# New cost numbers and block-border numbers for the planner that orders a two-layer encoder kernel on one TensorE-bound core

## The chip, the core and the metric

The kernel runs on one core of one Trainium2 chip. The metric is device time in microseconds (us) of one launch; lower is better. Three timed executions of the kernel before gave 1086.05, 1087.27 and 1087.64 us; the median is 1087.27 us.

A core has five engines with a queue of instructions each: PE (TensorE, matrix multiply; its weight loads are shown as PEld), DVE (VectorE), ACT (ScalarE), POOL (GpSimd) and SP (SyncE, which here only issues DMAs). Engines run side by side and wait for each other through semaphores. Within one engine, instructions run in the order in which they stand in its queue.

## What is computed

A trunk of two residual layers on a (512, 1024) float32 input, each with an RMS norm ahead of it, and one more RMS norm at the end:

```python
def even_layer(h, ...):          # layer 0
    xa, ba, ca, za, ub, vb, zb = split(h @ w_in)
    ya = short_conv_branch(xa, ba, ca, conv_w) * silu(za)
    yb = chunked_sgu_branch(ub, vb, ...) * silu(zb)
    return concat([ya, yb]) @ w_out

def odd_layer(h, ...):           # layer 1
    pc, zc, fd, zd = split(h @ w_in)
    yc = rwkv7_bidir_branch(pc, ...) * silu(zc)
    yd = fourier_branch(fd, fnet_w) * silu(zd)
    return concat([yc, yd]) @ w_out

def wkv7_step(state, inp):       # 512 positions, forward and backward, 16 heads of 64
    r, w, k, v, a, b = inp
    sa = einsum('ij,j->i', state, a)
    state = state * w + outer(sa, b) + outer(v, k)
    return state, einsum('ij,j->i', state, r)
```

## The kernel before, in words

**Arithmetic.** Large projections run as three rounded float32 matmuls: each operand is split into a high part `hh` and a low part `hl`, and high x high, high x low and low x high are summed (`mm3`, L551). One such matmul takes a 128x128 weight tile and 512 columns. Every weight block of 512 KB is loaded by SP into `wf_...` and split by two instructions in `splits` (L505): a cast makes the high half, on ACT or DVE, and a subtraction makes the low half, on POOL or DVE (`less`, with the gain `LO`).

**Layer 0** (up to about 455 us) is a row of such projections. **Layer 1** cuts the scan into 8 chunks of 64 positions for each of 8 pairs of heads (j = 0 to 7). For each j:
- `prep`, `half`: gates and scaled operands, on DVE, ACT and POOL;
- `scores`: three bursts of small matmuls (`sm`, `sa`, `sz`), masked by DVE and copied by ACT;
- `inverse`: a triangular inverse by blocks. PE has four bursts of 32x32 matmuls there: `iH` (64 matmuls, each float32 matmul is two records in the trace), then DVE adds a unit matrix to the result (`iHs`), then `iTT` (64) and `iTB` (32) need `iHs`; later `iG` (32) and `iTJ` (32);
- `fold`: `sp` (needs `iTT`, `iTJ`), copied to `pt`, and four bursts `sg`, which need `pt`; they are masked and copied into `gq`;
- `chain`: 8 steps of the scan. A step is one DVE multiply `X`, five to nine small PE matmuls into `pa` and eight into `py`; the next step's `X` needs `pa`.
Between these pieces the wide projections of layer 1 (`pd_k`, `pd_r`, `pd_v`, `pd_zc`, `pd_fd`, `pd_zd`) are laid in units of three matmuls, one `mm3` each. After the last step of the scan stand what is left of the output projection (`po`) and the final norm.

```python
        if op.eng == "PE" and op.mode != self.clock["mode"] and not s[3]:
            at += self.STAY
        if op.eng == "PE" and op.need > n and not op.glue:
            at = max(at, self.fetched.get(i + 1, t + self.FETCH) - op.cost * n / op.words)
```

The clock is used only while the program is built. [...] All instructions are recorded by one helper line (L401), so the profile's rows are told apart by tile names, not by lines.

## Time and profile before

| | |
|---|---|
| median of three timed executions | 1087.27 us (1086.05 to 1087.64) |
| the profiled execution's own time | 1090.07 us |
| its span, first to last instruction | 1088.3 us |
| PE, busy | 1024.3 us, 94%, 12024 matmul records |
| DVE, busy | 651.3 us, 60%, 1225 instructions |
| ACT, busy | 472.7 us, 43% |
| POOL, busy | 124.9 us, 11%, 155 instructions |
| DMA | 84 GB/s, mean over the span |

How to read it: the span is what the trace covers; the execution's own time is 1.8 us more, and 2.8 us over the median of the timed ones. PE is the busiest engine by far, so a microsecond in which PE has nothing to do, or runs slower, is where time can be won; an idle DVE or ACT costs nothing as such. "Busy" for PE counts a matmul from its start to its modelled end, and matmuls overlap, so costs on PE are better read from the distance between two starts.

### The profile page before, as it was taken

How to read it: one execution, taken by the hardware profiler on the slowest of the kernel's cores; microseconds unless marked ns; L12 is line 12 of the kernel's file. 1: busy time of each engine (PE TensorE's matmuls, PEld its weight loads, DVE VectorE, ACT ScalarE, POOL GpSimd, SP SyncE). 2: the span in 40 equal slices, each digit the busy share in tenths (PEclk: the TensorE clock that was granted, in tenths of full speed). 3: DMA queues.
4: the chain of work that ended last, by engine and by line, in shares of the span. 5: the costliest groups of instructions: out<-in, count | busy, mean ns of one | idle time of the engine just before them, and what ended most of it. 6: DMA issues, size and time to landing. Idle time of an engine off the chain costs nothing. (4 is left out here: it accounts for less than half of the span.)

```text
span 1088.3 us, 27301 instructions
## 1 busy us (share of the span) xinstructions
PE 1024.3 (94%) x12024; PEld 839.3 (77%) x12024; DVE 651.3 (60%) x1225; ACT 472.7 (43%) x795; POOL 124.9 (11%) x155
## 2 busy tenths in 40 slices
PE   7999999999999999998898999989988899999997
PEld 6988888888888888876676778767767677777776
DVE  6464444344343336895795858867793976864453
ACT  7232222222222125753565455744644736453253
POOL 1001210010110010220012101321021201110000
PEclk9999999999999999999998999989998999999999
DMA  8322222322223332332012011110121111154033
GB/s 286 105 73 94 81 94 98 97 97 97 96 96 124 130 116 98 100 105 89 8 46 89 3 42 61 49 52 21 41 71 41 60 39 48 60 172 131 30 107 117
DMA packets 32663, 91.51 MB, mean 84 GB/s; under 512 B 4896, under 2 KB 7712, under 8 KB 32544
## 3 DMA queue, kind: packets, MB, share of 16 engines
q1 hardware_dynamic: 32544, 89.77, 25.1%
q8 instruction: 94, 1.54, 0.6%
q14 instruction: 25, 0.20, 0.1%
HBM read 81.82 MB, written 7.86 MB: 82 GB/s over the span
## 5 line engine op out<-in xcount | busy, mean ns | idle before, releaser
L401 PE MATMUL pe<-w_e,yh 128*128 128x512 f32 x256 | 81.5, 398 | 0.0
L401 PE MATMUL sg<-ops 64*128 64x128 f32 x512 | 66.6, 294 | 7.2 <-ACT am L401 2.1
L401 PEld LDWEIGHTS sg<-ops 64*128 64x128 f32 x512 | 53.9, 196 | 17.1 <-issue 3.9
L401 PE MATMUL sg<-pt,am 64*128 64x128 f32 x512 | 60.5, 283 | 0.0
L401 PEld LDWEIGHTS pe<-w_e,yh 128*128 128x128 f32 x256 | 48.1, 188 | 11.6
L401 ACT COPY gq<-sg 128x256 f32<-128x256 f32 x64 | 23.2, 370 | 71.7 <-DVE gq L401 70.5
L401 PEld LDWEIGHTS sg<-pt,am 64*128 64x128 f32 x512 | 52.3, 195 | 0.0
L401 PE MATMUL pd_zc<-hh,w_zc 128*128 128x512 f32 x128 | 50.5, 437 | 1.3 <-DVE w_zc L401 1.3
L401 PE MATMUL pe<-w_e,yl 128*128 128x512 f32 x128 | 50.3, 393 | 0.0
L401 DVE TENSOR_TENSOR w_e<-wf_e,w_e 128x1024 fp32r<-128x1024 f32 (+1 forms) x19 | 20.0, 1074 | 48.0 <-ACT w_e L401 47.8
L401 PE MATMUL pd_r<-hh,w_r 128*128 128x512 f32 x128 | 45.5, 409 | 2.0 <-DVE w_r L401 2.0
L401 DVE TENSOR_TENSOR gq<-sg,c_masks 128x256 f32<-128x256 f32 x64 | 25.6, 416 | 33.7 <-PE sg L401 33.7
L401 PE MATMUL pd_k<-hh,w_k 128*128 128x512 f32 (+1 forms) x144 | 44.6, 372 | 0.0
L401 PEld LDWEIGHTS pa<-X,gq 128*64 128x64 f32 x448 | 30.8, 139 | 17.1 <-issue 3.9
L401 ACT CAST w_e<-wf_e 128x1024 fp32r<-128x1024 f32 (+1 forms) x19 | 16.9, 913 | 62.4 <-PE pe L401 54.6
L401 PE MATMUL pd_v<-hh,w_v 128*128 128x512 f32 x128 | 43.8, 410 | 0.0
L401 PE MATMUL pa<-X,gq 128*64 128x64 f32 x448 | 38.8, 230 | 4.6 <-DVE X L401 2.0
L401 PE MATMUL pa<-c_cen,vq 128*64 128x128 f32 x256 | 42.6, 288 | 0.0
L401 PE MATMUL pd_ub<-hh,w_ub 128*128 128x512 f32 x128 | 40.5, 393 | 0.0
L401 PE MATMUL pd_zb<-hh,w_zb 128*128 128x512 f32 x128 | 40.4, 392 | 0.0
L401 PE MATMUL pd_xa<-hh,w_xa 128*128 128x512 f32 x128 | 40.4, 392 | 0.0
L401 PE MATMUL pd_ca<-hh,w_ca 128*128 128x512 f32 x128 | 40.4, 392 | 0.0
(362 smaller groups left out, 2831.4 us busy)
## 6 DMA issues: line engine op xcount, KB each, us to landing
wf_e<-in_w_eo SPq DMA_DIRECT2D x16, 512.0 KB
wf_o<-in_w_oo SPq DMA_DIRECT2D x12, 512.0 KB
wf_pv<-in_w_ev SPq DMA_DIRECT2D x8, 512.0 KB
wf_ub<-in_w_e SPq DMA_DIRECT2D x8, 512.0 KB
wf_zb<-in_w_e SPq DMA_DIRECT2D x8, 512.0 KB
wf_xa<-in_w_e SPq DMA_DIRECT2D x8, 512.0 KB
wf_ca<-in_w_e SPq DMA_DIRECT2D x8, 512.0 KB
wf_za<-in_w_e SPq DMA_DIRECT2D x8, 512.0 KB
```

Of the source, the lines that this page charges most:

```text
L401: i = op.call(*op.a, **op.kw)
```

## The change

Only numbers of the planner change. The instructions and their operands are the same in number on PE (7720 matmuls, 12024 records); a few casts, copies and subtractions go to another engine, and the order changes on every engine from the first microseconds on.

```diff
--- before.py
+++ after.py
@@ -128,13 +128,13 @@
                 self.cost = n / 2250
             else:
                 self.cols *= 4
-                self.cost = n / (600 if aps[1].shape[0] > 64 else 1200) if m == P else 2 * max(m, n) / 1200 / {(P, 64): 1.7, (P, 32): 4, (64, 64): 4, (64, 32): 3}.get(self.mode, 2.5)
+                self.cost = n / (600 if aps[1].shape[0] > 64 else 1040) if m == P else 2 * max(m, n) / 1200 / {(P, 64): 1.75, (P, 32): 4, (64, 64): 3.9, (64, 32): 5}.get(self.mode, 3)
         elif eng == "Pool":
-            self.cost = 0.06 + n / {"tensor_tensor": 300, "tensor_scalar_mul": 228, "tensor_copy": 300}.get(name, 985)
+            self.cost = 0.06 + n / {"tensor_tensor": 300, "tensor_scalar_mul": 228, "tensor_copy": 900}.get(name, 985)
         else:
             more = sum(math.prod(x.shape[1:]) == 1 < n for x in self.ins) - (self.ins[0].space == PSUM if self.ins else 0) / 2
             rate = 500 if name in ("transpose", "tensor_tensor_scan") else 960
-            self.cost = {"DVE": 0.07 + n / rate + 0.06 * math.ceil(more), "ACT": 0.1 + n / 1200 + 0.09 * more, "SP": max(0.5, 0.06 + n / 720)}[eng]
+            self.cost = {"DVE": 0.1 + n / rate + 0.06 * math.ceil(more), "ACT": 0.14 + n / 1200 + 0.09 * more, "SP": max(0.5, 0.06 + n / 720)}[eng]
 
         banks = [(x.tensor.name, "bank") for x in self.outs + self.ins if x.space == PSUM]
         self.keys = [self.where(x) for x in self.outs] + [banks], [self.where(x) for x in self.ins]
@@ -162,10 +162,10 @@
 
 
     TICK, WINDOW, BUSY, SOFT = 3.413, 3.2, 4500.0, 2600.0
-    BLOCK, FIRST, READ, FETCH = 256, 178, 33, 3.6
-    SAFE, URGE, SWITCH, STAY, COLD = {}, 0.5, 0.2, 0.15, 2400.0
+    BLOCK, FIRST, READ, FETCH, MORE = 256, 194, 42, 3.6, 1 / 300
+    SAFE, URGE, SWITCH, STAY, COLD = {}, 0.5, 0.1, 0.0, 2800.0
     GIVE = {"PE": 0.15, "ACT": 0.1, "DVE": 0.15, "Pool": 9.0, "SP": 9.0}
-    SAME = {"DVE": 0.13, "ACT": 0.14, "Pool": 0.1}
+    SAME = {"DVE": 0.1, "ACT": 0.14, "Pool": 0.1}
     LATE = {"": 0.2, "PE": 0.25, "ACT": 0.2, "DVE": 0.3, "Pool": 0.3, "SP": 2.5}
 
     def __init__(self, tc, nc):
@@ -294,7 +294,7 @@
 
     def fetch(self, op):
 
-        self.issued += op.words
+        self.issued += op.words * (1 + self.MORE)
         while self.issued + self.READ >= self.block * self.BLOCK + self.FIRST:
             self.block += 1
             self.fetched[self.block + 1] = max(self.clock["PE"], self.fetched.get(self.block, 0.0)) + self.FETCH
@@ -411,7 +411,7 @@
             self.fill(s)
 
 
-LO, SLACK, BURST, ORDER = 0.5, 2, 1, (("v", 1), ("zc", 1), ("k", 2), ("r", 2))
+LO, SLACK, BURST, ORDER = 0.8, 2, 1, (("v", 1), ("zc", 1), ("k", 2), ("r", 2))
 FIRST = (("r", 0), ("v", 0), ("fd", 0), ("zd", 0), ("k", 1), ("fd", 1), ("r", 1), ("zd", 1), ("zc", 0))
 EXTRA = {0: (("fd", 2),), 3: (("zd", 2),), 5: (("fd", 3),), 6: (("zd", 3),)}
 FR, HL, XN, HH = 4, 0.6, 0.4, 0.5
```

`fetch` now counts 1/300 of a word more for each word issued (`MORE`), and the border is taken at 194 instead of 178, the start of a fetch 42 words ahead of it instead of 33. `STAY` is 0, so a change of tile shape is no longer shunned, and `SWITCH` is halved. DVE and ACT instructions are taken to be 0.03 and 0.04 us longer, bursts with a 64-row stationary tile and 128 columns 15% longer, 64x32 tiles shorter. `LO` goes from 0.5 to 0.8.

Over the whole program, POOL has 15 instructions more than before (six more low halves of layer 1's weights, three more of layer 0's, six more of the small `ll` halves), DVE's count is equal in sum, and ACT has 15 fewer. Changes of tile shape from one PE instruction to the next rise from 278 to 343.

PE, j = 5, from the end of `sa` to `iTT` and what follows. `iH5` is the burst whose result DVE turns into `iHs5`, `iTT5` the burst that reads it, `pd_r6` a wide projection. Before:

```order
L401 MATMUL sa5_11_8509<-ops3_3213,at5_1_8017 64x128
L401 MATMUL iH5_8550<-iD5_8527,off_103 32x32 x64
L401 MATMUL iTT5_8676<-iHs5_8551,iDt5_8528 32x32 x64
L401 MATMUL pd_r6_8562<-hh_84,w_r6_8547 128x512
L401 MATMUL pd_r6_8562<-hl_85,w_r6_8547 128x512
L401 MATMUL pd_r6_8562<-hh_84,w_r6_8548 128x512
```

and now:

```order
L401 MATMUL pd_k6_8678<-hh_84,w_k6_8613 128x512
L401 MATMUL iH5_8732<-iD5_8705,off_103 32x32 x64
L401 MATMUL pd_r6_8726<-hh_84,w_r6_8680 128x512
L401 MATMUL pd_r6_8726<-hl_85,w_r6_8680 128x512
L401 MATMUL pd_r6_8726<-hh_84,w_r6_8681 128x512
L401 MATMUL pd_r6_8726<-hh_84,w_r6_8680 128x512
L401 MATMUL pd_r6_8726<-hl_85,w_r6_8680 128x512
L401 MATMUL pd_r6_8726<-hh_84,w_r6_8681 128x512
L401 MATMUL pd_r6_8726<-hh_84,w_r6_8680 128x512
L401 MATMUL pd_r6_8726<-hl_85,w_r6_8680 128x512
L401 MATMUL pd_r6_8726<-hh_84,w_r6_8681 128x512
L401 MATMUL iTT5_8807<-iHs5_8733,iDt5_8706 32x32 x64
```

Before, `iTT5` stood right behind `iH5`; now nine wide matmuls stand between the two.

PE, j = 1 to 2, three bursts of small matmuls. `iTB1` and `iG1` belong to the inverse of pair 1, `sm2` to the scores of pair 2, `pd_v2`, `pd_k2` and `pd_r2` are wide projections. Before:

```order
L401 MATMUL pd_v2_5041<-hl_85,w_v2_4970 128x512
L401 MATMUL pd_v2_5041<-hh_84,w_v2_4971 128x512
L401 MATMUL iTB1_5053<-iDt1_4764,iHs1_4795 32x32 x32
L401 MATMUL iG1_5209<-dz1_3218,mt1_4352 32x32 x32
L401 MATMUL sm2_0_5244<-at2_0_4951,ops0_3204 32x64
```

and now:

```order
L401 MATMUL iTB1_4909<-iDt1_4733,iHs1_4764 32x32 x32
L401 MATMUL pd_k2_4497<-hh_84,w_k2_4457 128x512
L401 MATMUL pd_k2_4497<-hl_85,w_k2_4457 128x512
L401 MATMUL pd_k2_4497<-hh_84,w_k2_4458 128x512
L401 MATMUL iG1_5045<-dz1_3224,mt1_4247 32x32 x32
L401 MATMUL pd_k2_4497<-hh_84,w_k2_4457 128x512
L401 MATMUL pd_k2_4497<-hl_85,w_k2_4457 128x512
L401 MATMUL pd_k2_4497<-hh_84,w_k2_4458 128x512
L401 MATMUL pd_r2_4822<-hh_84,w_r2_4784 128x512
L401 MATMUL pd_r2_4822<-hl_85,w_r2_4784 128x512
L401 MATMUL pd_r2_4822<-hh_84,w_r2_4785 128x512
L401 MATMUL iTJ1_5085<-iG1s_5078,iB1_5039 32x32 x32
```

Before, `iTB1`, `iG1` and the 64 matmuls of `sm2` stood one behind the other; now three to six wide matmuls stand after each burst, and `sm2` comes later.

POOL, the preparation of pair 4 (`w4`, `a4`: gates; `ll`: low half of the small weights; `bon3`, `y2`: sums of earlier pairs; `w_v4`, `w_zc4`, `w_r4`: low halves of weight blocks). Before:

```order
L401 TENSOR_SCALAR w4_0_6307<-w4_0_6307 128x512
L401 TENSOR_TENSOR bon3_6360<-bon3_6360,rq3_1_5776 128x512
L401 TENSOR_TENSOR ll_104<-lora4_1_6704,lh4_1_6706 64x128
L401 TENSOR_SCALAR a4_0_6308<-a4_0_6308 128x512
L401 TENSOR_SCALAR w4_1_6723<-w4_1_6723 128x512
L401 TENSOR_TENSOR y2_6672<-y2_6672,bon2_5250 128x512
L401 TENSOR_SCALAR a4_1_6724<-a4_1_6724 128x512
L401 TENSOR_TENSOR w_v4_6783<-wf_v4_6754,w_v4_6782 128x1024
L401 TENSOR_TENSOR w_zc4_6840<-wf_zc4_6824,w_zc4_6839 128x1024
```

and now:

```order
L401 TENSOR_SCALAR w4_0_6607<-w4_0_6607 128x512
L401 TENSOR_SCALAR a4_0_6608<-a4_0_6608 128x512
L401 TENSOR_TENSOR ll_104<-lora4_1_6667,lh4_1_6669 64x128 x2
L401 TENSOR_TENSOR w_r4_6697<-wf_r4_6618,w_r4_6696 128x1024
L401 TENSOR_TENSOR bon3_6660<-bon3_6660,rq3_1_6040 128x512
L401 TENSOR_SCALAR w4_1_6708<-w4_1_6708 128x512
L401 TENSOR_SCALAR a4_1_6709<-a4_1_6709 128x512
L401 TENSOR_TENSOR w_v4_6795<-wf_v4_6742,w_v4_6794 128x1024
L401 TENSOR_TENSOR w_zc4_6930<-wf_zc4_6842,w_zc4_6929 128x1024
```

`w_r4` and a second `ll4_1` have come to POOL from DVE; `y2` has gone further ahead.

## The prediction

> **What bounds the kernel now.** I read the page first, for the engine that has least to spare, and then busy time by stage (columns: stretch and length in us; busy us and records of PE, PEld, DVE, ACT, POOL; granted clock; DMA share; GB/s).

> ```profile
> span 1088.3 us, 27301 instructions
> PE 1024.3 (94%) x12024; PEld 839.3 (77%) x12024; DVE 651.3 (60%) x1225; ACT 472.7 (43%) x795; POOL 124.9 (11%) x155
> ```
> ```profile
> 0.00:455.00 455.00, 447.49 (x2222) 377.73 (x2223) 211.12 (x290) 150.67 (x211) 41.88 (x47) 1.00 0.33 111
> 455.00:537.00 82.00, 72.94 (x1159) 56.44 (x1159) 61.64 (x117) 40.67 (x70) 11.79 (x20) 0.96 0.24 77
> 537.00:1036.00 499.00, 458.34 (x8446) 368.52 (x8446) 355.92 (x783) 258.77 (x476) 69.90 (x88) 0.97 0.18 58
> 1036.00:1088.00 52.00, 45.53 (x202) 36.64 (x202) 22.66 (x37) 22.62 (x39) 1.28 (x1) 0.97 0.32 111
> ```

> PE bounds the kernel. In layer 0 (first row) it stands idle for 7.5 us of 455, at the start, at full clock: no order can win much there. After the last step of the scan (last row) only wide `po` matmuls are left, and the idle 6.5 us are the final norm and store. So the change is decided between 455 and 1036 us, where PE is idle for 9.1 + 40.7 = 49.8 us and its clock is below 1. I then asked for the groups of PE instructions and for its waits, to see what the idle time is (group: records | busy us, mean ns | idle before, and what ended it; wait: us in total, times, longest).

> ```profile
> L401 PE MATMUL iTT<-iHs,iDt 32*32 32x32 f32 x1024 | 11.1, 199 | 10.3 <-DVE iHs L401 7.5 <-DVE zz L401 2.4 <-issue 0.5
> L401 PE MATMUL iH<-iD,off 32*32 32x32 f32 x1024 | 10.8, 194 | 3.3 <-issue 3.3
> L401 PE MATMUL iTB<-iDt,iHs 32*32 32x32 f32 x512 | 7.2, 204 | 3.3 <-issue 3.3
> ```
> ```profile
> PE sg L401 <- ACT am L401: 2.1, 3, 1.4
> PE sm L401 <- issue: 1.8, 1, 1.8
> PE sg L401 <- ACT dz L401: 1.7, 2, 1.2
> PE bo L401 <- issue: 0.5, 1, 0.5
> ```

> Two causes stand out, both at bursts of 32-wide matmuls: "issue", in which PE waits for no engine (3.3 + 3.3 + 0.5 + 1.8 + 0.5 = 9.4 us), and `iTT` waiting for DVE's `iHs` and `zz` (9.9 us). The rest is some 20 small waits of up to 2.5 us.

> **The change, term by term.** The sum is made against the profiled execution (1090.07 us, 1.8 of it outside the span) and then taken off the median of 1087.27 us, 2.8 us lower. No instruction is added on PE, and SP's loads are the same, so each term is idle time, clock or tile-shape changes.

> *Block borders.* Here is one "issue" stall in the timeline (start, length, form, records).

> ```profile
> 589.41 0.72 PE L401 MATMUL iTB<-iDt,iHs 32*32 32x32 f32 x62
> 589.94 0.23 PE L401 MATMUL iG<-dz,mt 32*32 32x32 f32 x2
> 589.95 0.21 PE L401 MATMUL iTB<-iDt,iHs 32*32 32x32 f32 x2
> 589.97 0.75 PE L401 MATMUL iG<-dz,mt 32*32 32x32 f32 x62
> 590.65 1.22 PE L401 MATMUL sm<-at,ops 64*32 64x64 f32 x59
> 593.63 1.30 PE L401 MATMUL sm<-at,ops 64*32 64x64 f32 x69 [1.76 <-issue]
> ```
> ```profile
> q8 instruction: 94, 1.54, 0.6%
> ```

> 187 records pass in 2.5 us, then PE stands in the middle of `sm`. PE's instructions come in 94 blocks of 1.54 MB / 94 = 16 KB, 256 words. Counted in the trace, all seven such stalls stand at word 192 to 194 of a block if each record is two words and each wait-only instruction one: 33 x 256 + 193 here. The old table leaves the wait-only words out and puts the border 178 words into the count of matmul words alone: 8 words late here, 46 at the last stall. The burst it thinks it has fitted then crosses the true border before the block is there. Reckoned from the record 42 words ahead of the border before, five of the seven stalls end after 3.5 to 3.9 us (here 589.75 to 593.63), two after 5.1 and 6.0. So I lay the true borders over both orders, and for each take the PE work from that record to the next border, at the trace's distances between starts. Before, 13 pieces hold less than 3.6 us, with a shortfall of 14 us in all, of which 9.4 show as "issue" and the rest lies under other waits. In the new order six do, with 3.1 us in all (worst: 2.3 us ahead of the border behind `sm7`). In proportion that leaves 9.4 x 3.1 / 14 = 2.1; with the two slow fetches in mind I take 2.4 left: **-7.0** (bounds: -6.3, all 3.1 seen, and -9.4).

> [...]

> *`iTT` behind `iH`.*

> ```profile
> 506.31 1.29 PE L401 MATMUL iH<-iD,off 32*32 32x32 f32 x128
> 510.29 1.29 PE L401 MATMUL iTT<-iHs,iDt 32*32 32x32 f32 x128 [2.70 <-DVE iHs L401]
> ```
> ```profile
> 713.86 0.68 DVE L401 TENSOR_TENSOR iHs<-iH,c_eye 128x512 f32<-128x512 f32 x1
> 714.68 1.28 PE L401 MATMUL iTT<-iHs,iDt 32*32 32x32 f32 x128 [3.28 <-DVE iHs L401]
> ```

> In pair 0 nothing stood between the two bursts, and `iTT` came 2.7 us late; in pair 3 six wide matmuls did, and it was still 3.3 us late, because DVE had other work ahead of `iHs`. The new order lays 9 to 12 wide matmuls there in seven of eight pairs (2.3 to 3.0 us of PE work; pair 4 has 8.8). Pairs 0, 1 and 5 are covered by that; pair 3 would still lack about 2 us (3.3 less the 1.3 us by which its cover grows), and I leave 0.9 for the others: 9.9 - 2.9, **-7.0** (bounds: 0, if DVE is late by as much elsewhere, and -9.9).

> *Half clock.*

> ```profile
> core 0: 1088.3 us, clock 0.983
> ```
> ```profile
> 500.00:520.00 20.00, 16.61 (x574) 12.90 (x572) 7.76 (x13) 9.73 (x19) 0.00 (x0) 0.91 0.21 67
> 580.00:600.00 20.00, 17.56 (x483) 13.90 (x483) 7.82 (x16) 9.87 (x19) 4.40 (x7) 0.75 0.27 83
> 820.00:840.00 20.00, 15.87 (x480) 12.97 (x480) 4.79 (x10) 6.58 (x13) 2.73 (x3) 0.83 0.17 54
> ```

> 0.017 x 1088.3 = 18.5 us are lost to a lower granted clock; I take 17 of them to lie ahead of the final norm. Nearly every one stands where dense 32-wide bursts and one of the stalls above follow each other (510.3, 593.6, 714.7 in the rows above). With wide matmuls between the bursts and no stall, I take two in five of them to go: **-7.0** (bounds: 0 and -17).

> *Changes of tile shape.*

> ```profile
> 533.77 0.39 PE L401 MATMUL pd_k<-hl,w_k 128*128 128x512 f32 x1
> 534.00 0.40 PE L401 MATMUL pd_k<-hh,w_k 128*128 128x512 f32 x1
> 534.32 0.65 PE L401 MATMUL pa<-c_cen,vq 128*64 128x128 f32 x4
> ```

> A wide matmul holds PE for 0.23 us, but 0.32 if the next has another shape: a change costs 0.09 to 0.10. The new order has 343 for 278: 65 x 0.097 = 6.3 us. Some fall into time in which PE would wait anyhow: **+5.0** (bounds 0 and +6.3).

> *`sg` behind `sp`.* In the new order the work between `sp` and the first `sg` that reads its copy is 1.0 to 1.3 us in four pairs, where one pair had so little before. In the old order such short covers cost either nothing or some 0.9 us, within the rows of `sg` above. Five places by 0.4: **+2.0** (bounds 0 and +4.5).

> *More halves on POOL.* Below are DVE's timeline, POOL's at the same time, and DVE's group of such halves.

> ```profile
> 707.09 0.68 DVE L401 TENSOR_TENSOR ops<-kq,a 128x512 f32<-128x512 f32 x1
> 708.35 2.94 DVE L401 TENSOR_TENSOR ops<-rq,E 128x512 f32<-128x512 f32 x2
> ```
> ```profile
> 707.77 2.37 POOL L401 TENSOR_TENSOR w_zc<-wf_zc,w_zc 128x1024 fp32r<-128x1024 f32 x1 [6.40 <-ACT w_zc L401]
> ```
> ```profile
> L401 DVE TENSOR_TENSOR w_k<-wf_k,w_k 128x1024 fp32r<-128x1024 f32 x8 | 9.8, 1226 | 0.6 <-ACT w_k L401 0.4 <-issue 0.2
> ```

> The first `ops` takes 0.68 us; the two that meet POOL's half take 2.94, some 1.6 us more. Six more halves of layer 1 go to POOL: each spares DVE 1.2 us and may block it for 1.6. Bounds: -7.3 (none meets) to +2.4 (all meet) on DVE, of which PE sees a part. Since the blocked work stood just ahead of the `iHs` that PE waited longest for, I take it near the upper end: **+2.0**.

> [...] Were every added half blocked for its own 2.4 us, this term would be 6 x 1.2 = +7.

> Sum: -7.0 - 7.0 - 7.0 + 5.0 + 2.0 + 2.0 = -12.0 us. 1087.27 - 12.0 = **1075.3 us**, 1078.1 for a profiled execution.

> **Rivals.** *DVE sets the pace (1085).*

> ```profile
> 537.00:615.00 78.00, 69.97 (x1230) 55.05 (x1232) 63.26 (x143) 44.36 (x82) 16.28 (x20) 0.93 0.15 48
> 615.00:667.00 52.00, 49.57 (x1112) 40.95 (x1109) 35.04 (x72) 28.70 (x53) 3.68 (x7) 1.00 0.15 45
> 667.00:742.00 75.00, 69.42 (x1235) 54.83 (x1232) 61.68 (x140) 42.11 (x80) 18.59 (x20) 0.95 0.14 43
> ```

> These are the steps of pairs 0, 1 and 2. PE idles 8.0 and 5.6 us where DVE is busy for 81 and 82% of the time, 2.4 where it is for 67%. At the trace's mean durations the new order puts 71 and 69 us of DVE's work beside 74 us of PE's into pairs 2 and 4, and 30 to 46 beside 41 to 57 into the others. If DVE can't get past 82%, these two last 87 and 84 us, 23 over PE's work; five others at 2.4 and the last at 2 make 37, against 40.7 now. That is -3.7; with -2 of half clock, -2.7 of the first `iTT` ahead of 537 us and +6.3 of changes it comes to -2: 1085.

> *Changes cost, waits move (1092).* If the waits taken from `iTT` and the borders only come back at `X`, `sg` and `sp`, the new order pays 65 x 0.097 = 6.3 us for nothing, less some 1.5 at borders: 1092. It is the slower side, decided in the wide blocks that are now cut up between the steps of the scan; it wins if waits and half clock together shrink by less than 6.3 us. For it speaks that only 19.3 of 49.8 us of idle time have a cause that the new order visibly attacks.

> *The border table doesn't fit (1082).* Its drift of 1/300 adds 80 words over the program, the new queue holds 98 wait-only ones. If its bursts stall after all, the first term is lost: 1082.

> *All of it works (1062).* Borders -9.4, `iTT` -9.9, half clock -17, other waits -2, less 6.3 and 7 for `sg` and POOL at their worst comes to -25: 1062.

> **Chances.** Forecast 0.50, DVE's pace 0.18, changes cost 0.17, border table 0.05, all of it 0.10. Under 0.2% (2.2 us) a measurement of this kernel hardly tells a difference from none. Faster by more: forecast, all of it, border table, and 0.11 of DVE's pace: 0.76. Same: the other 0.07. Slower: 0.17. The range runs from 1062 to 1091, which leaves some 0.1 on each side; the forecast's own is 1067 to 1082.

> **What would show it.** In the new profile PE's "issue" waits should be under 3.5 us and its waits of `iTT` for `iHs` under 3; the mean clock should be 0.989 or more; PE's idle time between the scan's first and last step should be under 34 us. DVE's pace shows as PE waiting for DVE in the steps of pairs 2 and 4; POOL's part as DVE's `ops` or `iA` over 1.5 us beside `w_...` halves. I am wrong if idle time stays at 41 us, or if new waits at `X`, `sg` or `sp` exceed 6 us.

## The result, and the profile after

The median falls from 1087.42 to 1061.81 us (1059.61 to 1063.80, four executions): a ratio of 0.977, interval 0.974 to 0.979, or 25.6 us. The direction was forecast, the size was not: -12 was the forecast, and the time is that of the rival in which all of it works (1062), though not by that rival's sum. Two of the later executions, one of only_border (1258 us) and one of no_vec (1242 us), ran at a mean clock of 0.75 and are left out of every figure below.

The first lines of the page after, then busy time by stage (columns as before; the scan's steps now run from 539 to 977 us, and ran from 537 to 1036), and the granted clock:

```profile
span 1061.9 us, 27323 instructions
PE 1020.0 (96%) x12024; PEld 823.1 (78%) x12024; DVE 661.5 (62%) x1225; ACT 470.7 (44%) x780; POOL 150.9 (14%) x170
```
```profile
0.00:455.00 455.00, 445.32 (x2213) 375.61 (x2214) 210.95 (x285) 148.84 (x206) 51.56 (x50) 1.00 0.33 111
455.00:537.00 82.00, 74.16 (x1163) 55.19 (x1163) 70.64 (x129) 44.77 (x77) 30.58 (x34) 0.96 0.23 78
537.00:977.00 440.00, 425.56 (x8324) 332.23 (x8321) 339.33 (x746) 241.49 (x441) 67.17 (x86) 1.00 0.17 57
977.00:1062.00 85.00, 74.98 (x334) 60.05 (x332) 40.62 (x67) 35.58 (x58) 1.58 (x1) 0.98 0.35 115
```
```profile
core 0: 1061.9 us, clock 0.994
```

Layer 0 is nearly as it was (idle for 9.7 us, 7.5 before). In the scan PE stands idle for 440.00 - 425.56 = 14.4 us, where it was 40.7, and its clock there is 1.00 for 0.97; the 82 us ahead of the scan, idle for 7.8, now lose more for each us than the scan does. The scan ends 59 us earlier, but not all of that is won: more of `po` is left for the stage behind it, which grows from 52 to 85 us and is idle for 10.0 us instead of 6.5. Over the whole span PE's idle time falls by some 22 us. The list of PE's waits shows what is left (rows picked: those for no engine, and some of the largest others of layer 1):

```profile
PE iH L401 <- DVE iD L401: 2.6, 1, 2.6
PE sm L401 <- DVE ops L401: 2.4, 2, 1.3
PE zw L401 <- ACT E L401: 2.2, 1, 2.2
PE iG L401 <- issue: 2.1, 3, 1.1
...
PE iTT L401 <- issue: 1.5, 2, 1.2
PE sg L401 <- ACT gq L401: 1.5, 2, 1.0
...
PE iTJ L401 <- issue: 0.8, 1, 0.8
PE py L401 <- issue: 0.6, 1, 0.6
...
PE ss L401 <- issue: 0.4, 1, 0.4
PE sm L401 <- issue: 0.4, 1, 0.4
...
PE pa L401 <- issue: 0.3, 1, 0.3
PE sp L401 <- issue: 0.2, 1, 0.2
PE sg L401 <- ACT am L401: 0.2, 1, 0.2
```

"issue" adds up to 6.2 us (unrounded; 9.3 before). No row of `iTT` waiting for `iHs` or `zz` is left (9.9 before). And `sg`, which the prediction took to get worse, got better. Its group before and, in the second fence, after (busy us, mean ns of one | idle us ahead of the group, and what ended it):

```profile
L401 PE MATMUL sg<-ops 64*128 64x128 f32 x512 | 66.6, 294 | 7.2 <-ACT am L401 2.1 <-ACT dz L401 1.7 <-ACT gq L401 1.3
```
```profile
L401 PE MATMUL sg<-ops 64*128 64x128 f32 x512 | 55.6, 285 | 1.6 <-ACT gq L401 1.5 <-ACT am L401 0.2
```

This is pair 0 in PE's timeline after, the place where `iTT` waited 2.70 us before:

```profile
508.90 0.80 PE L401 MATMUL iH<-iD,off 32*32 32x32 f32 x35
509.64 0.80 PE L401 MATMUL pd_zc<-hh,w_zc 128*128 128x512 f32 x1
...
513.52 0.40 PE L401 MATMUL pd_zc<-hh,w_zc 128*128 128x512 f32 x1
513.85 1.22 PE L401 MATMUL iTT<-iHs,iDt 32*32 32x32 f32 x121
516.30 0.23 PE L401 MATMUL iTT<-iHs,iDt 32*32 32x32 f32 x4 [1.23 <-issue]
516.38 0.74 PE L401 MATMUL iTB<-iDt,iHs 32*32 32x32 f32 x62
```

Wide matmuls cover DVE's `iHs`, and `iTT` waits for no engine; but a block border, at record 121 of `iTT`, still costs 1.23 us.

Where the 26.4 us between the two spans went, by these views (changes of shape are reckoned, not seen as time lost: how the sum of the usual distances between PE's starts differs between the two orders):

| term | forecast | measured |
|---|---|---|
| block borders ("issue" 9.3 to 6.2) | -7.0 | -3.1 |
| `iTT` behind `iH` (9.9 to 0) | -7.0 | -9.9 |
| half clock (0.017 x 1088.3 = 18.5 to 0.006 x 1061.9 = 6.4) | -7.0 | -12.1 |
| changes of tile shape (278 to 343) | +5.0 | +6.4 |
| `sg` (7.2 to 1.6) | +2.0 | -5.6 |
| POOL, and all other waits for DVE and ACT (46.5 to 28.3 in all) | +2.0 | -2.7 |
| sum | -12.0 | -27.0 |

So the sum closes within 1 us. The reckoned row agrees with the traces: PE's busy time less half of what it works at half clock is 1024.3 - 32.1 / 2 = 1008.3 us before and 1020.0 - 9.8 / 2 = 1015.1 after, 6.8 more. Three questions are left. What takes `sg`'s and the other waits away? Do the borders do what was said of them? And how much of this belongs to the numbers, how much to the one order that came out of them?

### The profile page after: what moved, and what is told of

It is laid out like the page before. It is cut to its first block, busy times and chain, and to the rows that moved or that the text cites. A ratio compares the mean times of both kernels' runs of the same rounds, so it can differ in the third digit from the quotient of the medians.

```text
span 1061.9 us, 27323 instructions
## 1 busy us (share of the span) xinstructions
PE 1020.0 (96%) x12024; PEld 823.1 (78%) x12024; DVE 661.5 (62%) x1225; ACT 470.7 (44%) x780; POOL 150.9 (14%) x170
## 3 DMA queue, kind: packets, MB, share of 16 engines
q8 instruction: 94, 1.54, 0.6%
## 4 chain that ended last, share of the span: by engine, by line
PE 84%; DVE 10%; ACT 2%; issue 2%; DMA 1%; SPq 1%; POOL 0%; DVEq 0%; ACTq 0%; POOLq 0%
PE pe L401 8%; PE po L401 6%; PE sg L401 5%; PE pv L401 4%; PE pd_zb L401 4%; PE pd_ub L401 4%; PE pd_xa L401 4%; PE pd_ba L401 4%; PE pd_za L401 4%; PE pd_ca L401 4%; PE pd_v L401 4%; PE pd_k L401 4%; PE pd_r L401 4%; PE pd_zc L401 3%; PE pa L401 3%
## 5 line engine op out<-in xcount | busy, mean ns | idle before, releaser
L401 PE MATMUL pe<-w_e,yh 128*128 128x512 f32 x256 | 81.0, 397 | 0.0
L401 PE MATMUL sg<-ops 64*128 64x128 f32 x512 | 55.6, 285 | 1.6 <-ACT gq L401 1.5
L401 PEld LDWEIGHTS pe<-w_e,yh 128*128 128x128 f32 x256 | 48.0, 188 | 11.6
L401 PE MATMUL sg<-pt,am 64*128 64x128 f32 x512 | 51.8, 273 | 0.0
L401 PEld LDWEIGHTS sg<-ops 64*128 64x128 f32 x512 | 41.8, 187 | 11.7 <-issue 7.0
L401 PE MATMUL pe<-w_e,yl 128*128 128x512 f32 x128 | 50.4, 394 | 0.0
L401 PE MATMUL pd_k<-hh,w_k 128*128 128x512 f32 (+1 forms) x144 | 49.1, 395 | 0.9 <-DVE w_k L401 0.9
L401 DVE TENSOR_TENSOR w_e<-wf_e,w_e 128x1024 fp32r<-128x1024 f32 (+1 forms) x19 | 20.0, 1074 | 48.0 <-ACT w_e L401 47.8
L401 PE MATMUL pd_zc<-hh,w_zc 128*128 128x512 f32 x128 | 49.0, 419 | 0.0
L401 PE MATMUL pd_r<-hh,w_r 128*128 128x512 f32 x128 | 48.2, 416 | 0.0
L401 PE MATMUL pd_v<-hh,w_v 128*128 128x512 f32 x128 | 46.1, 406 | 0.0
L401 ACT COPY gq<-sg 128x256 f32<-128x256 f32 x60 | 22.0, 371 | 51.6 <-DVE gq L401 51.4
L401 ACT CAST w_e<-wf_e 128x1024 fp32r<-128x1024 f32 (+1 forms) x19 | 16.9, 912 | 62.4 <-PE pe L401 54.5
L401 PE MATMUL pa<-c_cen,vq 128*64 128x128 f32 x256 | 41.9, 285 | 0.0
L401 PEld LDWEIGHTS sg<-pt,am 64*128 64x128 f32 x512 | 41.7, 188 | 0.0
L401 PE MATMUL pd_ub<-hh,w_ub 128*128 128x512 f32 x128 | 40.8, 394 | 0.0
L401 PE MATMUL pd_zb<-hh,w_zb 128*128 128x512 f32 x128 | 40.7, 394 | 0.0
L401 PE MATMUL pd_xa<-hh,w_xa 128*128 128x512 f32 x128 | 40.5, 392 | 0.0
L401 PE MATMUL pd_ba<-hh,w_ba 128*128 128x512 f32 x128 | 40.4, 392 | 0.0
L401 PE MATMUL pd_ca<-hh,w_ca 128*128 128x512 f32 x128 | 40.4, 392 | 0.0
L401 PE MATMUL pd_za<-hh,w_za 128*128 128x512 f32 x128 | 40.4, 392 | 0.0
L401 PEld LDWEIGHTS pa<-X,gq 128*64 128x64 f32 x448 | 30.3, 137 | 12.9 <-issue 3.5
```

The source lines that it names most:

```text
L401: i = op.call(*op.a, **op.kw)
```

## The experiments

Each kernel is the one before or the change with a few planner numbers different, or the change's own order with one thing edited. In the table, "waits" is the sum of the list of PE's waits for DVE and ACT, "half clock" is (1 - clock) x span; both are of one profiled execution. The ratio is of timed executions to those of the kernel before on the same chip. The kernel before itself had medians from 1087.4 to 1089.8 us on these chips, so small differences between rows are read from the ratios.

| kernel | ratio (interval) | median us | waits | issue | half clock | changes |
|---|---|---|---|---|---|---|
| before | | 1087.4 | 46.5 | 9.3 | 18.5 | 278 |
| the change | 0.977 (0.974-0.979) | 1061.8 | 28.3 | 6.2 | 6.4 | 343 |
| only_shape | 0.990 (0.987-0.994) | 1077.0 | 26.4 | 14.1 | 11.8 | 334 |
| no_shape | 1.023 (1.019-1.028) | 1112.9 | 58.0 | 8.0 | 33.3 | 273 |
| only_border | 0.993 (0.991-0.995) | 1080.6 | 49.0 | 3.3 | 12.9 | 264 |
| no_border | 0.980 (0.977-0.983) | 1065.4 | 27.8 | 9.6 | 7.4 | 330 |
| shape_border | 0.986 (0.981-0.992) | 1071.5 | 27.4 | 6.5 | 11.7 | 337 |
| f_shift | 0.982 (0.979-0.986) | 1070.9 | 26.8 | 10.7 | 9.6 | 344 |
| f_pool | 0.971 (0.967-0.975) | 1056.0 | 20.9 | 6.2 | 5.3 | 343 |
| n_before | 1.003 (1.000-1.006) | 1090.8 | 45.5 | 10.0 | 22.9 | 274 |
| n_before315 | 0.999 (0.997-1.001) | 1086.8 | 48.0 | 4.1 | 16.3 | 271 |
| n_after | 0.996 (0.993-0.998) | 1084.5 | 37.5 | 8.5 | 18.4 | 336 |
| n_after315 | 0.989 (0.985-0.994) | 1077.4 | 28.7 | 9.3 | 13.9 | 332 |
| n_after33 | 0.973 (0.968-0.977) | 1057.6 | 23.8 | 4.0 | 5.3 | 338 |
| no_vec | 0.986 (0.981-0.991) | 1072.2 | 32.6 | 3.5 | 10.7 | 349 |
| no_pe | 0.971 (0.967-0.976) | 1056.6 | 25.6 | 3.8 | 7.4 | 343 |
| n33_pool | 0.968 (0.964-0.972) | 1052.9 | 21.4 | 6.9 | 3.2 | 338 |
| n325_pool | 0.991 (0.988-0.994) | 1078.3 | 29.9 | 13.3 | 12.9 | 336 |

### Tile-shape numbers alone, and all but them

only_shape, on the kernel before; no_shape puts the old two values back into the change:

```diff
-    SAFE, URGE, SWITCH, STAY, COLD = {}, 0.5, 0.2, 0.15, 2400.0
+    SAFE, URGE, SWITCH, STAY, COLD = {}, 0.5, 0.1, 0.0, 2400.0
```

> The kernel before with SWITCH 0.1 and STAY 0 alone; all other numbers as before. Laid over this order, the true block borders leave a shortfall of 2.6 us (14.0 before, 3.1 in the changed kernel), and every pair has 2.3 to 2.8 us of PE work between iH and iTT; 334 changes of shape. Theory A (the border numbers took the issue stalls away, accurate durations the other waits): shape alone gains under 6 us, 1081 or more. Theory B (letting PE change shape freely lays wide matmuls between the dense bursts, and that takes the issue stalls, the iTT waits and the half clock away): 1072 or less, issue under 4 us, clock 0.990 or more. Theory C (luck of the order): anywhere from 1075 to 1095.

> The changed kernel with SWITCH 0.2 and STAY 0.15 put back. Shortfall at the borders 13.9 us, 273 changes of shape, no work between iH and iTT of pair 0. Theory A: keeps most of the gain, 1070 or less, issue under 4 us. Theory B: loses most of it, 1080 or more, issue 7 us or more, clock 0.986 or less. Theory C: anywhere from 1065 to 1095.

Alone, the two numbers win 1% and take the waits from 46.5 to 26.4 us. With 1077 us and 14.1 us of "issue" the run fits neither theory A nor B, only the wide range of luck. Without them the rest of the change is 2.3% slower than the kernel before, as theory B had it, and beyond the range of luck: waits 58.0 us, half clock 33.3. These are rows of PE's waits in no_shape, two of the tiles being those that the prediction feared for (`sg` and `sp`):

```profile
PE sp L401 <- ACT ysq L401: 3.3, 1, 3.3
PE sg L401 <- ACT dz L401: 2.9, 2, 1.5
PE sp L401 <- ACT am L401: 2.2, 2, 1.9
PE sa L401 <- ACT pt L401: 1.8, 2, 1.3
```

So the waits go with the two tile-shape numbers, and the rest of the table agrees: 45.5 to 58.0 us in the five kernels without them, 20.9 to 37.5 in the thirteen with them. The reading of it, from the orders, is that a planner that shuns changes lays small bursts side by side, and each waits for the mask or copy that follows the one ahead of it. Which of the two numbers does it was not tried. Why the other numbers without these two are worse than none was not settled; it is one order, too.

### Border numbers alone, all but them, and with the shape numbers

only_border, on the kernel before (no_border takes the same out of the change; shape_border is the kernel before with both):

```diff
-    BLOCK, FIRST, READ, FETCH = 256, 178, 33, 3.6
+    BLOCK, FIRST, READ, FETCH, MORE = 256, 194, 42, 3.6, 1 / 300
...
-        self.issued += op.words
+        self.issued += op.words * (1 + self.MORE)
```

> The kernel before with FIRST 194, READ 42 and the drift of 1/300 alone. Shortfall 13.6 us, 264 changes of shape. Theory A: issue under 4 us, 1080 or less. Theory B: issue stays near 9 us, 1083 to 1091.

> The changed kernel with FIRST 178, READ 33 and no drift. Shortfall 4.0 us, 330 changes of shape. Theory A: 5 to 7 us of issue come back, 1067 to 1070. Theory B: within 4 us of the changed kernel's 1062, issue under 7 us.

> The kernel before with SWITCH, STAY and the border numbers, and with all durations, LO and COLD as before. Theory B with the borders added: the two parts make most of the gain, 1068 or less, issue under 7 us. If the measured durations of DVE, ACT and the small groups carry what was won beyond the prediction: 1070 to 1078, with ACT and DVE waits as in the run with shape alone (26 us together) or more.

With the border numbers "issue" falls from 9.3 to 3.3 us alone, and is 9.6 without them, 6.2 with them, in the change. With the shape numbers it is 14.1 without and 6.5 with them. In these three pairs of orders that is 3 to 8 us of "issue" and 0.4% to 0.7% of the time. It is not shown that the border numbers did it: other orders of the same numbers, further down, scatter about as widely (4.1 to 10.0 us of "issue" with the old border numbers, 4.0 to 9.3 with the new ones). Of the expectations, only_border had the "issue" of theory A (under 4) and just missed its time (1080 or less), no_border the time of theory B (within 4 us of 1062) but more "issue", and shape_border fell into the case in which something else carries the rest. The old kind of order keeps its other waits: this is only_border.

```profile
PE iTT L401 <- DVE iHs L401: 4.8, 2, 2.9
PE iG L401 <- ACT dz L401: 2.9, 2, 1.7
PE iTT L401 <- DVE zz L401: 2.2, 1, 2.2
```

Both groups together win 1.4%, of the change's 2.3%. What gives the other 0.9% is open: `LO`, `COLD` and POOL's duration were not put back one by one, and one order may be that much better than another by chance.

### The borders moved through one order

f_shift keeps the change's order of every instruction and puts 32 tiny matmuls (64 records, 128 words, under 1 us at the 1.29 to 1.93 us that 128 such records take) ahead of PE's first transposes, into a tile that these overwrite, so that every border falls half a block elsewhere.

```diff
+            if op.name == "transpose" and not self.issued:
+                for _ in range(32):
+                    o, y, e = (v[0:32, 0:32] for v in op.a[:3])
+                    self.tc.keep_in_program_order(self.engines["PE"].matmul(o, e, y, start=True, stop=True))
```

> The changed kernel in exactly its order, with 32 tiny 32x32 matmuls (64 records, 128 words) put ahead of the first transposes, so that every block border stands 128 words earlier in the work; the results are overwritten. The start grows by under 2 us. If borders decide by where they fall, 'issue' rises from 6.2 to 10 us or more and the time by 3 to 8 us over the changed kernel beside the start. If they hardly matter as long as wide work lies between the bursts, 'issue' stays within 2 us of 6.2 and the time within 2 us.

"issue" rises from 6.2 to 10.7 us and the span by 6.5, as expected if borders decide by where they fall. PE's timeline in pair 0 of f_shift, the piece shown above for the change:

```profile
514.52 1.27 PE L405 MATMUL iTT<-iHs,iDt 32*32 32x32 f32 x127
...
515.62 0.68 PE L405 MATMUL iTB<-iDt,iHs 32*32 32x32 f32 x56
519.18 0.26 PE L405 MATMUL iTB<-iDt,iHs 32*32 32x32 f32 x7 [2.88 <-issue]
```

The stall now comes 127 + 1 + 1 + 56 = 185 records into the bursts instead of 121. The 64 records that were put in bring every border 64 records forward, to 57, and the next one stands a block of 128 records behind it, at 185. In both kernels the stall ends 4.2 to 4.4 us after PE passed the border ahead; here all 128 records between the two borders are of dense bursts, so PE is through them sooner and waits longer (2.88 us for 1.23). So "issue" is the block border, shown at equal order.

### POOL's halves on DVE

f_pool keeps the change's order and issues the eleven low halves of layer 1's weights, which POOL computes there, on DVE:

```diff
-            i = op.call(*op.a, **op.kw)
+            call = op.call
+            if op.eng == "Pool" and op.name == "tensor_tensor" and re.match(r"w_(k|r|v|zc|fd|zd)\d", op.a[0].tensor.name):
+                call = self.engines["DVE"].tensor_tensor
+            i = call(*op.a, **op.kw)
```

> The changed kernel in its order, but the 11 low halves of layer 1's weights that the planner gave to POOL are issued on DVE at the same place. DVE gets 11 x 1.22 = 13.4 us of work more and POOL 26 us less. If POOL's halves block DVE about as long as they spare it (the prediction's term), the time changes by under 3 us either way. If they are real relief for DVE, it rises by 6 us or more, with PE's waits for DVE. If blocking costs more than it spares, it falls by 3 us or more.

Faster by 5.8 us by the medians and 0.6% by the ratios, as expected if blocking costs more than it spares, though DVE gets eleven instructions of 1.2 to 1.6 us more. DVE and POOL of the change, and then the same DVE instruction in f_pool (start, length):

```profile
850.33 2.29 DVE L401 TENSOR_TENSOR iA<-iA,iT 128x64 f32<-128x64 f32 x1
```
```profile
850.18 2.36 POOL L401 TENSOR_TENSOR w_k<-wf_k,w_k 128x1024 fp32r<-128x1024 f32 x1
```
```profile
843.21 0.22 DVE L404 TENSOR_TENSOR iA<-iA,iT 128x64 f32<-128x64 f32 x1
...
845.25 1.59 DVE L404 TENSOR_TENSOR w_k<-wf_k,w_k 128x1024 fp32r<-128x1024 f32 x1
```

A DVE instruction of 0.22 us takes 2.29 us and ends with POOL's half. Over the whole program, the time of DVE's instructions that overlap one of POOL's, above the median of the same form without overlap, sums to some 25 us before, 45 in the change and 27 in f_pool. The halves on POOL cost more than they spare.

### Is it the numbers, or the draw of one order?

`WINDOW`, the length over which the planner counts columns, stays put in the change. Moving it by 2 or 3% means nothing to the chip, but gives another order of the same kind. n_before and n_before315 do this to the kernel before, n_after, n_after315 and n_after33 to the change (3.25, 3.15 and 3.3):

```diff
-    TICK, WINDOW, BUSY, SOFT = 3.413, 3.2, 4500.0, 2600.0
+    TICK, WINDOW, BUSY, SOFT = 3.413, 3.25, 4500.0, 2600.0
```

> The changed kernel with one number that means nothing here set a little otherwise (WINDOW 3.25 for 3.2), which gives another order of the same kind: 336 changes of shape, 2.5 to 3.0 us between iH and iTT. If the gain lies in the kind of order, 1058 to 1070, clock 0.990 or more, ACT waits under 10 us. If it is luck of one order, 1070 or more.

> The kernel before with the number that means nothing (WINDOW 3.25 for 3.2): another order of the old kind, 274 changes of shape. If the kind of order decides: 1080 to 1105, half clock 14 us or more. If luck decides as much: it may reach 1070.

> The kernel before with WINDOW 3.15: a third order of the old kind, 271 changes of shape. If the kind decides: 1080 to 1105. If luck decides as much: it may reach 1070.

> The changed kernel with WINDOW 3.15: a third order of the new kind, 332 changes of shape, 2.9 to 3.0 us between iH and iTT. If the changed kernel's 1062 is a lucky draw of its kind: 1066 to 1086, half clock 10 us or more. If the kind gives it and WINDOW 3.25 was an unlucky draw: 1058 to 1066.

> The changed kernel with WINDOW 3.3: a fourth order of the new kind, 338 changes of shape. The same two cases as with 3.15: 1066 to 1086 if 1062 was a lucky draw, 1058 to 1066 if not.

The three orders of the old numbers lie within 4 us. The four of the new ones have ratios of 0.973, 0.977, 0.989 and 0.996: all faster, mean 0.984 (-18 us), spread over 25 us, which leaves the mean uncertain by some 6 us. Of the cases expected, n_after and n_after315 (1084.5 and 1077.4 us) say that the change's 1062 was a lucky draw, and n_after33 (1057.6) that it was not. In all four `iTT` waits for no engine; what differs is "issue", half clock and PE's waits, `iH` among them (2.6 us in the change, 4.8 to 7.2 in the others). This is the worst place in n_after (PE's timeline; then busy time and clock of that stretch):

```profile
902.92 1.93 PE L401 MATMUL iH<-iD,off 32*32 32x32 f32 x128 [4.20 <-DVE iD L401]
904.78 1.22 PE L401 MATMUL pd_v<-hh,w_v 128*128 128x512 f32 x2
...
914.40 0.66 PE L401 MATMUL sm<-at,ops 64*32 64x64 f32 x40
917.08 1.55 PE L401 MATMUL sm<-at,ops 64*32 64x64 f32 x88 [2.03 <-issue]
918.56 0.79 PE L401 MATMUL pd_v<-hh,w_v 128*128 128x512 f32 x1
```
```profile
900.00:920.00 20.00, 14.89 (x534) 12.01 (x535) 7.89 (x15) 5.17 (x9) 1.00 (x4) 0.67 0.21 69
```

`iH` waits 4.2 us, and behind it PE works at half clock: 128 records take 1.93 us where they take 1.29 at full clock, and wide matmuls stand 0.43 us apart for 0.23. Then three bursts side by side cross a border, with a stall of 2.03 us, and wide matmuls behind it stand 0.43 us apart again. One stretch of 20 us loses 5.1 us to waits and at most 6.6 to the clock (0.33 x 20; by the trace PE waits for some 4 us of the half-clock time anyhow, which leaves 4.6). Over the 18 kernels of the table a fit gives 0.59 us of half clock more for each us of PE's waits more, issue counted (correlation 0.92): by that, a wait taken away would be worth some 1.6 times its length. A fit of the span itself gives 1.3 us for each us of waits (correlation 0.97); the orders with fewer waits have more changes of tile shape, which may be why it is less. No run takes a single wait away, so this is how the two go together, not a price that was shown.

### Duration numbers, and POOL's halves in a good and a bad draw

no_vec and no_pe put the old durations of DVE and ACT, or of small PE groups, back into the change; n33_pool and n325_pool are n_after33 and n_after with the edit of f_pool.

```diff
-            self.cost = {"DVE": 0.1 + n / rate + 0.06 * math.ceil(more), "ACT": 0.14 + n / 1200 + 0.09 * more, "SP": max(0.5, 0.06 + n / 720)}[eng]
+            self.cost = {"DVE": 0.07 + n / rate + 0.06 * math.ceil(more), "ACT": 0.1 + n / 1200 + 0.09 * more, "SP": max(0.5, 0.06 + n / 720)}[eng]
...
-    SAME = {"DVE": 0.1, "ACT": 0.14, "Pool": 0.1}
+    SAME = {"DVE": 0.13, "ACT": 0.14, "Pool": 0.1}
```

> The change without its longer durations of DVE and ACT instructions (and with the old number for waits of one engine for itself). If these numbers carry the fall of PE's waits for DVE and ACT (29 us in the change, 46.5 before): such waits of 36 us or more and a time of 1075 to 1090. If they do not: waits of 22 to 33 us and a time within the scatter of the new kind about its middle, 1058 to 1075. Shortfall at block borders is 3.0 us by the order, so issue stalls of 4 to 9 us either way.

> The change with the old durations of small matmul groups. If the durations of small groups carry part of the gain: 1075 to 1090, with PE's waits for DVE and ACT at 36 us or more. If not: within 1055 to 1075, waits of 22 to 33 us. By the order alone its shortfall at block borders is the smallest seen (1.5 us), so issue stalls of 3 to 8 us.

> The change with the planner's window number at 3.3 (1057.6 us alone) and, in that exact order, the eleven low halves of layer 1's weights issued on DVE in place of POOL. [...] Rival (the gain seen in the order of the change was that order's own luck): within 2 us of 1057.6, or slower, since eleven halves of 1.2 us each are added to DVE.

> The same edit in the order of the window number 3.25 (1084.5 us alone, the slowest of the new kind; DVE's delay under POOL 48 us). Theory (a constant cost of POOL's halves): faster by 3 to 10 us, 1074.5 to 1081.5, and still at least 15 us slower than the good draw with the same edit, since its block borders and half clock stay. Rival (POOL's halves are what makes this draw slow): faster by 15 us or more, under 1069.5. Second rival (luck of one order): within 2 us of 1084.5 or slower.

Neither group of durations carries the fall of the waits: 32.6 us without the one, 25.6 without the other, both times in the ranges expected for that case and about the scatter of the new kind (no_pe is as fast as any order of the change without the POOL edit). The POOL edit gains 5.8, 4.7 and 6.2 us by the medians in three orders (6.3, 4.7 and 4.8 by the ratios; each is about as large as its interval, but all three agree), while the distance between a good and a bad draw stays: 1052.9 and 1078.3 with it, 1057.6 and 1084.5 without. So the halves on POOL are not what makes draws bad, and no difference in their cost between the orders is seen. In n33_pool and n325_pool (not in f_pool) "issue" rises with the edit (4.0 to 6.9 and 8.5 to 13.3 us), though PE's order and its borders are the same: where PE waits less for DVE, it comes to the next border sooner. That is a reading, not tried. n33_pool, 3.2% under the kernel before, is the fastest of all.

## Why the prediction fell short

**`sg` behind `sp`, and the waits that no term names: the step that failed.** The prediction counted in how many pairs the work between `sp` and the first `sg` had become short, and put +2.0 on it. Measured: 7.2 to 1.6, -5.6. All the waits that it doesn't name it left as they were; with POOL's term they were to be +2.0 and came out at -2.7. These two make 12.3 of the 15.0 us by which the sum missed. The count looked at one cover and missed that the copies `sg` waited for before (`am`, `dz`, `gq`) are covered too, once small bursts no longer stand side by side. The runs name what does it: the two tile-shape numbers alone take 20 us of waits away, PE's waits are low wherever these numbers are in, and `sg` waits for engines for 5.4 to 8.6 us in the five kernels without them and for 0.4 to 3.6 in the thirteen with them. The rival "changes cost, waits move" made the same error in words: it held it for a point that only 19.3 us of idle time have a cause that the new order visibly attacks.

**Half clock: right direction, too small.** Two in five of 17 us were put down to go; two in three went (-12.1). It was tied to the stalls named. The other waits fell as well, and over the 18 kernels half clock goes with all of PE's waits; that it fell because of them fits, but no run separates the two.

**`iTT` behind `iH`: right, and whole.** All 9.9 us went, for 7.0. The 2.9 us left for pair 3 and the rest did not come: DVE was done with `iHs` 0.7 to 1.8 us after the end of `iH` in every pair, where pair 3 took 4.8 before, and 9 to 12 wide matmuls cover that. DVE's own order has a part in it: in no_vec three pairs are late again (3.4 to 3.9 us), and `iTT` waits for 2.9.

**Block borders: the stall is real, the count of it is not borne out.** -3.1 for -7.0; 6.2 us of "issue" against the 2.4 expected and the 3.5 set as a mark. That the stalls stand at the true borders is right, as f_shift shows (6.2 to 10.7 us in the same order). The step that failed in this term is the fixed 3.6 us for a fetch: by that count only_shape should lose 2.6 us, and it lost 14.1. Over the eight orders whose count is on record, the shortfall counted and "issue" don't go together (13.6 and 3.3 us in only_border, 3.1 and 6.2 in the change). So this term's sign was in good part luck.

**Changes of tile shape** cost +6.4 for +5.0, by the reckoning above: nearly nothing fell into waiting time. **More halves on POOL** were rightly a cost. f_pool gives 5.8 us for eleven halves, so an estimate of 3 us for the six that were added, if each costs the same; in the measured sum this hides under waits that fell by more.

**Rivals.** These are the steps of pairs 2 and 4 after, where DVE's pace was to show:

```profile
642.00:725.00 83.00, 78.98 (x1404) 60.88 (x1404) 74.46 (x151) 48.45 (x85) 20.89 (x22) 0.98 0.18 56
769.00:850.00 81.00, 76.56 (x1390) 58.58 (x1388) 70.40 (x154) 46.88 (x81) 17.06 (x21) 1.00 0.18 58
```

DVE gets past the 82% at which that rival held it: 90 and 87% here, and PE idles for 4.0 and 4.4 us. Most of the scan's idle time is in these two pairs and the one behind them, but it is a third of the 23 us that the rival gave the two. Whether the border table fits stays open: "issue" is 6.2 us, between the 2.4 of the forecast and the 9.4 of that rival. What the prediction had no case for is the draw: its -12 stands beside a mean of -18 over four orders of these numbers, with single orders from -5 to -30. By that mean some 8 us of the 25.6 are this order's luck, give or take the 6 us by which four orders leave the mean uncertain; for the numbers as a kind, -12 is not ruled out.

**The marks.** Clock 0.994 (0.989 or more asked for), `iTT`'s waits for `iHs` 0 (under 3), idle time in the scan 14.4 us (under 34): met. "issue" 6.2 (under 3.5): missed. New waits at `X`, `sg` or `sp` of over 6 us did not come (`sg` 1.6 in all, `sp` none, `pa` for `X` 1.4). DVE's instructions beside POOL's halves: seen, at 2.29 us.

## What to carry to other kernels

When an order changes as a whole, price the waits that it doesn't name as well: take the tiles at which the critical engine waits now and look at what each has ahead of it in the new order, instead of leaving them as they are. Where waits and a lowered clock stand together, count a wait at more than its length (over the 18 kernels here the span went by 1.3 us with each us of waits). And before a gain is put down to a planner's numbers, nudge one that means nothing: here that moved the time by up to 27 us, as much as the change itself, and "issue" by more than 5 us.

## What the runs showed of the hardware

- **Blocks of instructions.** Queue q8 moved 94 pieces of 16 KB (1.54 MB), and in f_shift a stall stood 128 records behind the border ahead of it. The planner's fixed 3.6 us for a fetch was not borne out: in only_shape eleven of thirteen stalls ended 3.4 to 5.1 us after the border ahead of theirs (one after 5.8, one after 2.3), and the order, due 2.6 us of stalls by 3.6 us for each fetch, had 14.1. These times are worked out from the trace's records of single instructions and transfers. The longest stall there is 2.6 us, and 2.9 in f_shift. Before and after the change, all 18 of PE's stalls of 0.2 us or more that waited for no engine ended 1.2 to 1.5 us after the end of a q8 transfer.
- **Half clock** (a granted clock of 0.5), as the traces record it ahead of the final norm, came in pieces of 3.4 us or a multiple of it (before: four of 3.4 and three of 6.8; after: three of 3.4; in the other runs mostly 3.4, often 6.8, and 10.2 in n_after and in no_shape). Wide matmuls stood 0.43 us apart in them, 0.23 at full clock. In all 18 traces PE has a stall of 0.7 to 4.2 us in the 7 us ahead of each piece, often with bursts of 32-wide matmuls about it, but not always.
- **POOL and DVE.** Beside one 128x1024 subtraction on POOL (2.36 us) an instruction on DVE took 2.29 us; it took 0.22 in f_pool, where that subtraction was not on POOL.
